# Log-sum-exp on one core: a second part of 16 rows per partition read last, the first logarithms held behind row 118, and more rows summed one by one

## The chip, the cores and the metric

The kernel runs on one core of a Trainium2 chip. The metric is the device time of one execution, in microseconds (us), the median of several runs. A profile is one further execution with the hardware profiler on; its span goes from the first to the last instruction, and some time lies around it.

## The reference

For each of 32 x 512 = 16384 rows of 1024 fp32 values the kernel computes the logarithm of the sum of exponentials:

```
max_x = np.max(x, axis=-1, keepdims=True)
return (max_x.squeeze(-1) + np.log(np.sum(np.exp(x - max_x), axis=-1))).astype(np.float32)
```

The input is 67.1 MB, drawn from a normal distribution. The output has 16384 fp32 values, 64 KB.

## The kernel before

The 16384 rows are spread over 128 partitions, 128 rows (columns of `sumexp`) to each. The kernel takes the exponentials without subtracting the maximum, sums them and takes the logarithm; beside this it finds out whether any sum left the range 1e-15 to 1e15, and only if one did does a second, careful pass run (the branch at L200, not taken with this input).

The rows lie in two parts of the input. `x_rest` has the last B = 8 rows per partition, `x_rows` the other W = 120. In either part a partition's rows are contiguous, so partitions begin 120 x 4 KB = 480 KB apart in the first and 32 KB apart in the second.

A list of 17 loads sets everything. Each load brings some rows of all partitions into the next free slots of a ring of 48 row slots in SBUF; when a load does not fit behind the last, it begins at slot 0 again. SyncE (SP) issues all loads on one queue (L90). Loads 2, 3 and 4 are issued as 4, 2 and 2 transfers, so that there are 22 in all. A transfer waits until the slots' former rows have been used, and the eight semaphores used for transfers are taken in turn, so that a transfer also waits until the eighth before it has landed.

The list gives each load's operations. A letter and a number stand for so many rows:

- `R8`: ScalarE takes the exponential of 8 rows in place (L133), and VectorE sums them with one reduction (L140).
- `T3`: ScalarE takes the exponential of 3 rows in place (L133), and VectorE sums row by row, with one instruction that adds the two halves of a row and sums the result (L145).
- `A`: ScalarE takes the exponential of one row and sums it in the same instruction (L131); VectorE has nothing to do.

The order of the instructions on each engine is made by a scheduler of the framework, which may put an instruction earlier than the program has it, and it makes the semaphore waits between engines from what each instruction reads and writes. Where the program knows a wait to be unneeded, it says so (`without_wait`).

Around the loads there are these steps:

- L162: the logarithms of the first EARLY = 104 columns, on ScalarE; L182: those of the last 24.
- L163 and L164: `check` of the first LATE = 118 columns: VectorE clamps the sums (L102), counts those that differ (L106), and TensorE adds the count into one PSUM value (L110). L188 does the same for columns 118 to 126.
- L183 and L184: two stores on SyncE's queue, first the 8 columns of `x_rest` (32 bytes per partition), at the end the 120 of `x_rows` (480 bytes). Load 7 is the one that reads `x_rest` (REST = 7), and its sums lie in columns 0 to 7.
- L189 to L195: VectorE looks at a part of the last row, TensorE adds this (L193) and the last row's sum (L194) to the count, and VectorE makes a flag of it (L195). ScalarE and VectorE load the flag and branch (L196 to L200). At L264 all engines finish together.

Of the kernel before, what the change touches and what calls it, by code (L numbers as in the profile page):

```python
# [14 lines left out]
def kernel(  # L15
# [5 lines left out]
    nc = tc.nc  # L21
# [3 lines left out]
    AF = mybir.ActivationFunctionType  # L25
# [6 lines left out]
    NC = n // P  # L32
# [2 lines left out]

    B = 8
    W = NC - B
    x_rows = x_flat[0 : P * W].rearrange("(p c) d -> p c d", p=P)  # L40
    x_rest = x_flat[P * W : n].rearrange("(p c) d -> p c d", p=P)
    out_flat = out.rearrange("a b -> (a b)")
    out_rows = out_flat[0 : P * W].rearrange("(p c) -> p c", p=P)
    out_rest = out_flat[P * W : n].rearrange("(p c) -> p c", p=P)
# [3 lines left out]

    RING = 48
    loads = [  # L50
        "R8 R8", "R8 R8", "R8 R8", "R7 R6 A A", "R6 R5 A A A", "R5 R4 A", "R5 R4", "R5 T3",
        "R3 A A A", "R3 A", "R2 T2", "R3", "R1 A", "T2", "T1", "A", "A",
    ]
    loads = [[(op[0], int(op[1:] or 1)) for op in load.split()] for load in loads]
    assert sum(s for ops in loads for _, s in ops) == NC
    ENGINES = [mybir.EngineType.Activation, mybir.EngineType.DVE]
    REST = 7
    EARLY = 104
    LATE = 118
    LAST = NC - 1  # L60

# [4 lines left out]
    ring = big.tile([P, RING, d], fp32, name="ring")  # L66
    sumexp = stats.tile([P, NC], fp32, name="sumexp")
    res = stats.tile([P, NC], fp32, name="res")
# [10 lines left out]
    nc.vector.memset(far, 100 * HIGH)  # L79

    def source(c0, size):
        assert c0 >= B or (c0 == 0 and size == B)
        return x_rows[:, c0 - B : c0 - B + size, :] if c0 >= B else x_rest

    def load(p0, c0, size, i):


        step = {2: 4, 3: 2, 4: 2}.get(i, 1)
        return [
            nc.sync.dma_start(  # L90
                out=ring[k::step, p0 : p0 + size, :], in_=source(c0, size)[k::step]
            ).ins
            for k in range(step)
        ]

    def without_wait(ins, group, reason):

        tc.declare_no_dep(ins.ins, group=group, reason=reason)


    def check(c0, c1, i):
        nc.vector.tensor_scalar(  # L102
            out=clamped[:, c0:c1], in0=sumexp[:, c0:c1],
            scalar1=LOW, scalar2=HIGH, op0=ALU.max, op1=ALU.min,
        )
        nc.vector.scalar_tensor_tensor(  # L106
            out=clamped[:, c0:c1], in0=clamped[:, c0:c1], scalar=0.0, in1=sumexp[:, c0:c1],
            op0=ALU.bypass, op1=ALU.not_equal, accum_out=bad[:, i : i + 1],
        )
        nc.tensor.matmul(count, lhsT=bad[:, i : i + 1], rhs=far, start=i == 0, stop=False)  # L110

    following = B
    p = 0
    for i, ops in enumerate(loads):
        size = sum(s for _, s in ops)
        if p + size > RING:
            p = 0
        if i == REST:
            c = 0
        else:  # L120
            c = following
            following += size
        dmas = load(p, c, size, i)
        if i == 0:
            first_load = dmas[0]
        for how, s in ops:
            v = ring[:, p : p + s, :]
            sums = sumexp[:, c : c + s]
            if how == "A":
                o = v if c < LAST else last_exp  # L130
                exp = nc.scalar.activation(out=o, in_=v, func=AF.Exp, accum_out=sums)  # L131
            else:
                exp = nc.scalar.activation(out=v, in_=v, func=AF.Exp)  # L133
            without_wait(exp, "loads", "the slot's earlier users came before this load")
            without_wait(exp, "exps", "the slot's earlier users came before this load")
            without_wait(exp, "sums", "the slot's earlier users came before this load")
            tc.add_to_no_dep_group("exps", exp.ins)
            added = []
            if how == "R":
                added = [nc.vector.reduce_sum(out=sums, in_=v, axis=AX.X)]  # L140
            elif how == "T":
                for r in range(s):
                    lo = ring[:, p + r, 0:H]
                    added.append(
                        nc.vector.scalar_tensor_tensor(  # L145
                            out=lo, in0=lo, scalar=1.0, in1=ring[:, p + r, H:d],
                            op0=ALU.mult, op1=ALU.add, accum_out=sums[:, r : r + 1],
                        )
                    )
            for add in added:  # L150
                for dma in dmas:
                    tc.declare_no_dep(add.ins, dma, reason="ScalarE has waited for it")
                without_wait(add, "loads", "they came before this one")
            for add in added:
                tc.add_to_no_dep_group("sums", add.ins)
            c += s
            p += s
            last_row = v
        for dma in dmas:
            tc.add_to_no_dep_group("loads", dma)  # L160
        if following == EARLY + 14:
            nc.scalar.activation(out=res[:, 0:EARLY], in_=sumexp[:, 0:EARLY], func=AF.Ln)  # L162
        if following == LATE + 3:  # L163
            check(0, LATE, 0)  # L164

    def start_early(program):

# [11 lines left out]

    nc.at_finalize(start_early)  # L180

    nc.scalar.activation(out=res[:, EARLY:NC], in_=sumexp[:, EARLY:NC], func=AF.Ln)  # L182
    nc.sync.dma_start(out=out_rest, in_=res[:, 0:B])  # L183
    nc.sync.dma_start(out=out_rows, in_=res[:, B:NC])  # L184

    check(LATE, LAST, 1)  # L188
    nc.vector.reduce_max(out=bad[:, 3:4], in_=last_row[:, 0, 0 : d // 16], axis=AX.X)  # L189
    nc.vector.tensor_scalar(  # L190
        out=bad[:, 2:3], in0=bad[:, 3:4], scalar1=LOG_LOW, scalar2=None, op0=ALU.is_lt
# [8 lines left out]
    with tc.If(all_fine < 1, preferred_fallthrough_block=False):  # L200
        with tc.tile_critical(sync_engine=mybir.EngineType.Activation):
            with nc.semaphore("landed") as landed, nc.semaphore("ready") as ready:
                rows = 0
                steps = 0
                for c0 in range(0, NC, RING):
                    s = min(RING, NC - c0)
                    v = ring[:, 0:s, :]
                    neg = clamped[:, c0 : c0 + s]
                    if c0:
                        nc.scalar.wait_ge(ready, steps)  # L210
                    for c1, s1 in ((0, B), (B, s - B)) if c0 == 0 else ((c0, s),):
                        nc.scalar.dma_start(
                            out=ring[:, c1 - c0 : c1 - c0 + s1, :], in_=source(c1, s1)
                        ).then_inc(landed, 16)
                        rows += 16
                    nc.vector.wait_ge(landed, rows)
                    nc.vector.tensor_reduce(
                        out=neg, in_=v, op=ALU.max, axis=AX.X, negate=True
                    ).then_inc(ready, 1)
                    nc.vector.wait_ge(ready, steps + 1)  # L220
                    nc.vector.tensor_add(
                        out=v, in0=v, in1=neg[:, :, None].to_broadcast([P, s, d])
                    ).then_inc(ready, 1)
                    nc.scalar.wait_ge(ready, steps + 2)
                    nc.scalar.activation(out=v, in_=v, func=AF.Exp).then_inc(ready, 1)
                    nc.vector.wait_ge(ready, steps + 3)
                    nc.vector.reduce_sum(
                        out=sumexp[:, c0 : c0 + s], in_=v, axis=AX.X
                    ).then_inc(ready, 1)
                    steps += 4  # L230
                nc.scalar.wait_ge(ready, steps)
                nc.scalar.activation(out=res, in_=sumexp, func=AF.Ln).then_inc(ready, 1)
                nc.vector.wait_ge(ready, steps + 1)
                nc.vector.tensor_sub(out=res, in0=res, in1=clamped).then_inc(ready, 1)
                nc.scalar.wait_ge(ready, steps + 2)
                nc.scalar.dma_start(out=out_rest, in_=res[:, 0:B]).then_inc(landed, 16)
                nc.scalar.dma_start(out=out_rows, in_=res[:, B:NC]).then_inc(landed, 16)
                nc.scalar.wait_ge(landed, rows + 32)


# [28 lines left out]
```

## Time and profile before

| | us |
|---|---|
| median of 4 runs | 163.75 (163.71 to 163.83) |
| the profiled execution | 163.94 |
| its span | 162.1 |
| VectorE busy | 122.4 (75%) |
| ScalarE busy | 116.8 (72%) |
| first exponential starts | 22.16 |
| last exponential starts | 158.30 |
| last logarithms start (L182) | 159.48 |
| final store (L184) issued | 159.73, lands 1.6 later |

The page's row of DMA tenths shows 40 equal slices of the span; a 9 is a slice in which the DMA engines were at least 90% busy. A group of instructions is shown by line, engine, operation, output and input, shape and count, then busy time and the mean length of one in ns, then the idle time of the engine just before them and what ended it. In a timeline a line begins with its start and length in us; the bracket tells how long the engine was idle before it and what it waited for. Neighbouring instructions of one form are merged into one line with their count.

### The profile page before, as it was taken

To read this page: it belongs to the slowest core of one execution; us is meant where nothing else is said; L and a number is where in the kernel's file an instruction comes from. 1 tells how busy PE (TensorE), PEld (TensorE's weight loads), DVE (VectorE), ACT (ScalarE), POOL (GpSimd) and SP (SyncE) were. 2 spreads that over 40 slices of the span, in tenths; PEclk is the share of its full clock that TensorE was granted. 3 is DMA by queue.
4 is the path that set the end of the run, shared out by engine and by line. 5 is a ranking of instruction groups with operands and counts; after the bars stand their busy time and mean duration, and the time that the engine had idled before them with its cause. 6 is when DMAs were issued, how large, how long until landed. Compare 5 with 4: busy or idle time off the path is not lost.

```text
span 162.1 us, 216 instructions
## 1 busy us (share of the span) xinstructions
PE 0.6 (0%) x8; PEld 0.3 (0%) x8; DVE 122.4 (75%) x47; ACT 116.8 (72%) x53; POOL 0.2 (0%) x4
## 2 busy tenths in 40 slices
PE   0000000000000000000000000000000000000001
PEld 0000000000000000000000000000000000000000
DVE  0000000799949999499999995999998999979993
ACT  3000059990799609994499839999969599999993
POOL 0000000000000000000000000000000000000000
DMA  8995996997997999699999979899999999999980
GB/s 259 517 517 259 517 517 275 501 517 307 469 517 340 437 501 470 273 470 485 453 453 453 439 338 434 384 443 437 437 412 485 398 418 416 437 409 417 417 329 17
DMA packets 2817, 67.18 MB, mean 414 GB/s; under 512 B 640, under 2 KB 640, under 8 KB 1024
## 3 DMA queue, kind: packets, MB, share of 16 engines
q1 hardware_dynamic: 2816, 67.18, 96.9%
q14 instruction: 1, 0.01, 0.0%
HBM read 67.11 MB, written 0.07 MB: 414 GB/s over the span
## 4 chain that ended last, share of the span: by engine, by line
DMA 63%; DVE 22%; ACT 12%; issue 0%; SPq 0%; PE 0%; DVEq 0%; ACTq 0%
DMA ring<-in_x_dram 63%; DVE sumexp L140 21%; ACT ring L133 12%; DVE ring L145 1%; SPq L90 0%; PE count L193 0%; DVE clamped L102 0%; DVE bad L190 0%; DVE bad L189 0%; DVE clamped L106 0%; DVE fine L195 0%; PE count L194 0%; DVEq L102 0%; ACTq L133 0%
## 5 line engine op out<-in xcount | busy, mean ns | idle before, releaser
L140 DVE TENSOR_REDUCE sumexp<-ring 128x8 f32<-128x8192 f32 (+7 forms) x20 | 116.2, 5855 | 36.1 <-ACT ring L133 36.1
L133 ACT ACTIVATE ring<-ring 128x8192 f32<-128x8192 f32 (+7 forms) x24 | 101.8, 4284 | 42.1 <-DMA ring<-in_x_dram 42.0
L131 ACT ACTIVATE ring<-ring 128x1024 f32<-128x1024 f32 x12 | 12.5, 1041 | 0.0
L145 DVE SCALAR_TENSOR_TENSOR ring<-ring 128x512 f32<-128x512 f32 x8 | 5.1, 687 | 0.0
L131 ACT ACTIVATION_READ_ACCUMULATOR ring<-ring 128x1 f32 x12 | 2.2, 187 | 0.0
L77 ACT ACT_TABLE_LOAD x1 | 1.3, 1283 | 0.8 <-PEq L253 0.8
L131 ACT ACTIVATE last_exp<-ring 128x1024 f32<-128x1024 f32 x1 | 1.0, 1027 | 0.0
L110 PE MATMUL count<-far,bad 128*1 128x1 f32 x4 | 0.4, 164 | 159.0 <-DVE clamped L106 159.0
L78 DVE MEMSET ones<- 128x1 f32 x1 | 0.1, 59 | 0.9 <-PEq L253 0.9
L145 DVE DVE_READ_ACCUMULATOR ring<-ring 128x1 f32 x8 | 0.7, 85 | 0.0
L106 DVE SCALAR_TENSOR_TENSOR clamped<-clamped,sumexp 128x118 f32<-128x118 f32 (+1 forms) x2 | 0.5, 226 | 0.1
L102 DVE TENSOR_SCALAR clamped<-sumexp 128x118 f32<-128x118 f32 (+1 forms) x2 | 0.4, 198 | 0.1
L110 PEld LDWEIGHTS count<-far,bad 128*1 128x1 f32 x4 | 0.2, 80 | 159.1 <-DVE clamped L106 159.1
L195 DVE TENSOR_SCALAR fine<-count 1x1 int32<-1x1 f32 x1 | 0.1, 146 | 0.3 <-PE count L194 0.3
L162 ACT ACTIVATE res<-sumexp 128x104 f32<-128x104 f32 x1 | 0.3, 273 | 0.0
L182 ACT ACTIVATE res<-sumexp 128x24 f32<-128x24 f32 x1 | 0.2, 223 | 0.0
L189 DVE TENSOR_REDUCE bad<-ring 128x1 f32<-128x64 f32 x1 | 0.2, 219 | 0.0
L193 PE MATMUL count<-far,bad 128*1 128x1 f32 x2 | 0.2, 164 | 0.2 <-DVE bad L190 0.2
L194 PE MATMUL count<-ones,sumexp 128*1 128x1 f32 x2 | 0.2, 163 | 0.0
L131 ACT ACTIVATION_READ_ACCUMULATOR last_exp<-ring 128x1 f32 x1 | 0.2, 186 | 0.0
L190 DVE TENSOR_SCALAR bad<-bad 128x1 f32<-128x1 f32 x1 | 0.2, 153 | 0.0
L106 DVE DVE_READ_ACCUMULATOR clamped<-clamped,sumexp 128x1 f32 x2 | 0.2, 84 | 0.0
(7 smaller groups left out, 0.7 us busy)
## 6 DMA issues: line engine op xcount, KB each, us to landing
ring<-in_x_dram SPq DMA_DIRECT2D x2, 3840.0 KB, 27.7
ring<-in_x_dram SPq DMA_DIRECT2D x2, 3584.0 KB, 25.6
ring<-in_x_dram SPq DMA_DIRECT2D x1, 5120.0 KB, 31.3
ring<-in_x_dram SPq DMA_DIRECT2D x1, 4608.0 KB, 33.7
ring<-in_x_dram SPq DMA_DIRECT2D x1, 4096.0 KB, 29.3
ring<-in_x_dram SPq DMA_DIRECT2D x2, 2048.0 KB, 32.7
ring<-in_x_dram SPq DMA_DIRECT2D x1, 3072.0 KB, 36.2
ring<-in_x_dram SPq DMA_DIRECT2D x2, 1024.0 KB, 38.8
```

The costliest lines, as they stand in the source:

```text
L77: nc.scalar.preload_act_table_set("natural_log_exp_and_others")
L102: nc.vector.tensor_scalar(out=clamped[:, c0:c1], in0=sumexp[:, c0:c1], scalar1=LOW, scalar2=HIGH, op0=ALU.max, op1=ALU.min,)
L106: nc.vector.scalar_tensor_tensor(out=clamped[:, c0:c1], in0=clamped[:, c0:c1], scalar=0.0, in1=sumexp[:, c0:c1], op0=ALU.bypass, op1=ALU.n ...
L110: nc.tensor.matmul(count, lhsT=bad[:, i : i + 1], rhs=far, start=i == 0, stop=False)
L131: exp = nc.scalar.activation(out=o, in_=v, func=AF.Exp, accum_out=sums)
L133: exp = nc.scalar.activation(out=v, in_=v, func=AF.Exp)
L140: added = [nc.vector.reduce_sum(out=sums, in_=v, axis=AX.X)]
L145: nc.vector.scalar_tensor_tensor(out=lo, in0=lo, scalar=1.0, in1=ring[:, p + r, H:d], op0=ALU.mult, op1=ALU.add, accum_out=sums[:, r : r + 1],
L162: nc.scalar.activation(out=res[:, 0:EARLY], in_=sumexp[:, 0:EARLY], func=AF.Ln)
L182: nc.scalar.activation(out=res[:, EARLY:NC], in_=sumexp[:, EARLY:NC], func=AF.Ln)
L189: nc.vector.reduce_max(out=bad[:, 3:4], in_=last_row[:, 0, 0 : d // 16], axis=AX.X)
L190: nc.vector.tensor_scalar(out=bad[:, 2:3], in0=bad[:, 3:4], scalar1=LOG_LOW, scalar2=None, op0=ALU.is_lt)
```

## The change

Five things are changed.

- B is 16 instead of 8, W 112 instead of 120, so partitions begin 448 KB apart in the first part and 64 KB apart in the second. Columns are now read in order, 0 to 127: the second part is columns 112 to 127 and is read last, by loads 9 to 16, where it was load 7.
- The list of loads is another: five loads of 16 rows and then 12, 8, 6, 6, 3, 3, 3, 2, 2, 1, 1, 1, where it was three of 16 and then 15, 14, 10, 9, 8, 6, 4, 4, 3, 2, 2, 1, 1, 1. 17 rows are summed one by one on VectorE (T) where 8 were, 10 on ScalarE (A) where 13 were.
- The first logarithms are those of 112 columns instead of 104. A new function, `in_this_order`, fixes an order on one engine without a wait: the logarithms stand behind the exponential of row 118 and ahead of the next one.
- The `check` of the first 118 columns is put ahead of the next sum on VectorE in the same way.
- The first store is that of the 112 columns of `x_rows` (448 bytes per partition), the final one that of the 16 of `x_rest` (64 bytes).

The branch that is not taken is changed to match.

```diff
-    B = 8
+    B = 16
...
     loads = [
-        "R8 R8", "R8 R8", "R8 R8", "R7 R6 A A", "R6 R5 A A A", "R5 R4 A", "R5 R4", "R5 T3",
-        "R3 A A A", "R3 A", "R2 T2", "R3", "R1 A", "T2", "T1", "A", "A",
+        "R6 R5 R5", "R6 R5 R5", "R8 R8", "R8 R8", "R4 R4 R3 R3 A A", "R6 T3 T3", "R6 A A", "T4 T2",
+        "R3 R3", "R3", "A A A", "R2 A", "T2", "T2", "T1", "A", "A",
     ]
...
-    REST = 7
-    EARLY = 104
     LATE = 118
...
-        assert c0 >= B or (c0 == 0 and size == B)
-        return x_rows[:, c0 - B : c0 - B + size, :] if c0 >= B else x_rest
+        assert c0 >= W or c0 + size <= W
+        return x_rest[:, c0 - W : c0 - W + size, :] if c0 >= W else x_rows[:, c0 : c0 + size, :]
...
+    def in_this_order(first, then):
+
+        info = mybir.DependencyInfo(mybir.DependencyClass.NoSync, mybir.DependencyReason.DATA)
+        tc.add_manual_dep(then.ins, first.ins.name, info, reason="order on one engine")
...
+            if ln:
+                in_this_order(ln, exp)
+                ln = None
...
+                if counted:
+                    in_this_order(counted, add)
+                    counted = None
...
-        if following == EARLY + 14:
-            nc.scalar.activation(out=res[:, 0:EARLY], in_=sumexp[:, 0:EARLY], func=AF.Ln)
-        if following == LATE + 3:
-            check(0, LATE, 0)
+        if c == LATE:
+            ln = nc.scalar.activation(out=res[:, 0:W], in_=sumexp[:, 0:W], func=AF.Ln)
+            in_this_order(exp, ln)
+            counted = check(0, LATE, 0)
...
-    nc.scalar.activation(out=res[:, EARLY:NC], in_=sumexp[:, EARLY:NC], func=AF.Ln)
-    nc.sync.dma_start(out=out_rest, in_=res[:, 0:B])
-    nc.sync.dma_start(out=out_rows, in_=res[:, B:NC])
+    nc.scalar.activation(out=res[:, W:NC], in_=sumexp[:, W:NC], func=AF.Ln)
+    nc.sync.dma_start(out=out_rows, in_=res[:, 0:W])
+    nc.sync.dma_start(out=out_rest, in_=res[:, W:NC])
```

More of the change, by code (lines that the diff above doesn't have):

```diff
@@ L105, in check @@
         )
-        nc.vector.scalar_tensor_tensor(
+        counted = nc.vector.scalar_tensor_tensor(
             out=clamped[:, c0:c1], in0=clamped[:, c0:c1], scalar=0.0, in1=sumexp[:, c0:c1],
@@ L110, in check @@
         nc.tensor.matmul(count, lhsT=bad[:, i : i + 1], rhs=far, start=i == 0, stop=False)
-    following = B
+        return counted
+    ln = counted = None
+    c = 0
     p = 0
@@ L117 @@
             p = 0
[L118 to L122, printed above, removed]
         dmas = load(p, c, size, i)
@@ L210 @@
                         nc.scalar.wait_ge(ready, steps)
-                    for c1, s1 in ((0, B), (B, s - B)) if c0 == 0 else ((c0, s),):
+                    edge = max(c0, min(W, c0 + s))
+                    for c1, c2 in ((c0, edge), (edge, c0 + s)):
+                        if c1 == c2:
+                            continue
                         nc.scalar.dma_start(
-                            out=ring[:, c1 - c0 : c1 - c0 + s1, :], in_=source(c1, s1)
+                            out=ring[:, c1 - c0 : c2 - c0, :], in_=source(c1, c2 - c1)
                         ).then_inc(landed, 16)
@@ L235 @@
                 nc.scalar.wait_ge(ready, steps + 2)
-                nc.scalar.dma_start(out=out_rest, in_=res[:, 0:B]).then_inc(landed, 16)
-                nc.scalar.dma_start(out=out_rows, in_=res[:, B:NC]).then_inc(landed, 16)
+                nc.scalar.dma_start(out=out_rest, in_=res[:, W:NC]).then_inc(landed, 16)
+                nc.scalar.dma_start(out=out_rows, in_=res[:, 0:W]).then_inc(landed, 16)
                 nc.scalar.wait_ge(landed, rows + 32)
```

## The prediction

> **What bounds the kernel now.** I read the page's line of busy DMA tenths and its queue line first, then the stages, then ScalarE's order of time from 119 us on, then what SyncE waits for at the end.
>
> ```profile
> DMA  8995996997997999699999979899999999999980
> q1 hardware_dynamic: 2816, 67.18, 96.9%
> ```
> ```profile
> 22.00:61.00 39.00, 0.00 (x0) 0.00 (x0) 29.70 (x4) 27.95 (x5) 0.00 (x0) 1.00 0.99 429
> 119.00:141.00 22.00, 0.00 (x0) 0.00 (x0) 21.54 (x11) 20.08 (x10) 0.00 (x0) 1.00 1.00 427
> 141.00:158.00 17.00, 0.19 (x2) 0.09 (x2) 15.78 (x17) 16.73 (x15) 0.00 (x0) 1.00 0.97 401
> 158.00:162.10 4.10, 0.43 (x6) 0.22 (x6) 1.43 (x10) 1.68 (x5) 0.00 (x0) 1.00 0.06 17
> ```
>
> In a stage line the columns after the length are PE, PEld, DVE, ACT and POOL busy, the clock, the DMA share and GB/s. The 16 DMA engines are full (0.97 to 1.00) in every stage until 158; of the 162.1 us the stream takes 157. So only three things can move the time: the stream itself, how far ScalarE and VectorE trail its last row, and the 4 us after it.
>
> ```profile
> 22.16 13.95 ACT L133 ACTIVATE ring<-ring 128x8192 f32<-128x8192 f32 x2 [20.08 <-DMA ring<-in_x_dram]
> 41.51 13.95 ACT L133 ACTIVATE ring<-ring 128x8192 f32<-128x8192 f32 x2 [5.40 <-DMA ring<-in_x_dram]
> 119.00 7.98 ACT L133 ACTIVATE ring<-ring 128x5120 f32<-128x5120 f32 x2 [1.27 <-DMA ring<-in_x_dram]
> 128.72 7.12 ACT L133 ACTIVATE ring<-ring 128x5120 f32<-128x5120 f32 x2 [1.75 <-DMA ring<-in_x_dram]
> 136.02 2.76 ACT L133 ACTIVATE ring<-ring 128x3072 f32<-128x3072 f32 x1 [0.18 <-DMA ring<-in_x_dram]
> 154.49 2.86 ACT L133 ACTIVATE ring<-ring 128x2048 f32<-128x2048 f32 x2 [0.23 <-DMA ring<-in_x_dram]
> 157.25 1.04 ACT L131 ACTIVATE ring<-ring 128x1024 f32<-128x1024 f32 x1
> 158.30 1.03 ACT L131 ACTIVATE last_exp<-ring 128x1024 f32<-128x1024 f32 x1
> 159.48 0.22 ACT L182 ACTIVATE res<-sumexp 128x24 f32<-128x24 f32 x1
> ```
>
> Each bracketed wait ends as a load lands, so differences of starts give the stream's law: 16 rows per partition 41.51 - 22.16 = 19.35 us, 6 rows 136.02 - 128.72 = 7.30 us, hence 1.205 us a row and 0.07 us a load. The last exponential starts at 158.30, straight behind its predecessor, and the trace's record of the last load's landing is 158.28: ScalarE arrives exactly as the data does.
>
> **The change, part by part.**
>
> *The stream.* Both schedules have 17 loads in 22 transfers, and both have brought 118 rows with load 10; from there both go 3, 2, 2, 1, 1, 1. By the law, row 118 lands at the same 145.8, the later loads at 149.5, 152.0, 154.5, 155.7, 157.0 and 158.3. Price 0, provided that each load is issued before the queue runs dry. The slots of the ring decide that, worked out with these prices (mean ns in the last but one place):
>
> ```profile
> L140 DVE TENSOR_REDUCE sumexp<-ring 128x6 f32<-128x6144 f32 x2 | 13.1, 6550 | 2.0 <-ACT ring L133 2.0
> L131 ACT ACTIVATE ring<-ring 128x1024 f32<-128x1024 f32 x12 | 12.5, 1041 | 0.0
> L133 ACT ACTIVATE ring<-ring 128x3072 f32<-128x3072 f32 x4 | 11.0, 2756 | 0.2 <-DMA ring<-in_x_dram 0.2
> L140 DVE TENSOR_REDUCE sumexp<-ring 128x3 f32<-128x3072 f32 x3 | 10.1, 3353 | 1.2 <-ACT ring L133 1.2
> L145 DVE SCALAR_TENSOR_TENSOR ring<-ring 128x512 f32<-128x512 f32 x8 | 5.1, 687 | 0.0
> ```
>
> From start to start they are a little shorter: an R6 sum 6.47, an R3 sum 3.27, a row summed alone 0.61 (138.63 to 139.24), exponentials 2.66 for three rows, 1.81 for two, 1.04 with their own sum. Load 5 (12 rows) needs load 2's two sums, which end at 85.4 as before; the stream wants it at 99.5. Load 6 needs load 3's first sum, 95.9, and is wanted at 114.0; load 7, 104.5 against 123.8; the last four wait for load 5's R6, 126.1, against 152. One more wait is SyncE's eight semaphores: a transfer waits for the eighth before it, so load 16 for load 8 (138.4, wanted at 157). Margins are 14 us and more: nothing shows.
>
> *Where the rows lie.* Partitions of the first part now begin 448 KB apart, not 480; those of the second 64 KB, not 32. The row that bears on this is the 8 rows before 128.72, the old second part: 9.72 us, where the law gives 9.71. Two very different distances agree within 0.1%, so I take 0, with 0.1% of the stream's 155 us, 0.16 us, either way. The Trainium skill, DMA: Bandwidth & Descriptors, section "Latency and other measured facts", speaks against the change: it has copies at a row pitch of 512 KiB at 207 GB/s where a padded layout reaches 214, blames large powers of two, and 448 KB is a multiple of 64 KB. If that 3% held here the time would be some 5 us longer; no run here shows such a loss.
>
> *ScalarE at the end.* Load 8 (R3 R3) lands at 138.40 and finds it idle. Then three R3 exponentials end at 146.40, A A A at 149.52, the 112 logarithms (0.18 until the next start, as the 104 took at 141.81) at 149.70, R2 151.51, A 152.55, T2 154.36. Load 13 lands at 154.48. From there the sequence T2, T1, A, A is the old one, so the last exponential again starts at 158.30. The cover is 0.13 us of idle time before load 13; any more delay than that goes one for one into the end.
>
> *What the logarithms wait for.* They need VectorE's sums through row 111 and stand in ScalarE's order, so a late sum holds up every exponential behind them, then VectorE's sums of those. VectorE by the prices above: load 4's four sums end at 119.65, R6 126.12, six single rows 129.78, R6 (its exponential ends at 129.95) 136.44, six single rows 140.1, then R3 from 141.2 to 144.47 and R3 to 147.8. That is 1.7 us before 149.52: price 0. The R3 of load 9 runs until 151.1, and the logarithms must not wait for it. The old ones started at 141.81 while a sum of rows they did not need ran from 140.46 to 143.8, so waits go by rows.
>
> *VectorE at the end.* The comparison of 118 rows (0.6 us) waits for load 10's A A A too (149.6, long past) and goes from 151.1 to 151.7; behind it stand R2, to 153.9, and nothing that ScalarE or a load waits for; T2 at 154.5 and T2 at 156.4 find it idle; T1 ends at 158.34 instead of 158.62. The nine single rows that replace sums of blocks cost 0.61 instead of 1.07 each, but in idle time.
>
> *The stores.* The first store now carries 448 bytes a partition and is queued behind all loads, as the 32-byte one was (16.4 us to landing); its eight packets an engine follow the last load and are done near 158.5, before the final store's first packet at 160.57. The final store shrinks from 480 to 64 bytes. In the packet records a 480-byte packet takes 26 ns and a 32-byte one 9; eight of each follow one another, 0.21 or 0.07 us. I take the nearer, 9: it lands 0.14 us earlier than 161.31; the bounds are 0 and 0.14.
>
> *What is late next.* SyncE's last waits:
>
> ```profile
> SPq L264 <- DVEq L200: 0.4, 1, 0.4
> SPq L264 <- DMA out_dram<-res: 0.3, 1, 0.3
> SPq L264 <- ACTq L200: 0.3, 1, 0.3
> ```
>
> The store's wait is only 0.3 us beyond the branch, and VectorE leaves the branch late: its closing drain is recorded at 161.35 to 161.40, SyncE's at 161.45. VectorE's side hangs on the flag, on PE L194, on the last sum at 159.46; PE's L193, until now held to 159.51 by VectorE's chain from the T rows, comes 0.27 us earlier, so L194 ends some 0.06 earlier. The closing barrier then follows 161.35 (VectorE) instead of 161.45: 0.10 us saved, not 0.14. Bounds 0 and 0.14.
>
> **Sum.** The profiled execution took 163.94 us, 162.1 in its span and 1.84 around it: 163.94 - 0.10 = 163.84. It lies 0.19 above the runs' median, so against that 163.75 - 0.10 = **163.65**. Less than 0.2% (0.33 us), about what a measurement of this kernel can tell from no change.
>
> **Rivals.**
> 1. *The logarithms wait for row 114* (slower). If the wait covers the R3 of load 9, ScalarE stands until 151.1, R2 ends at 153.1, A 154.1, T2 155.95, and load 13 starts 1.45 us after its landing; nothing behind it is idle, so the end moves by that: 163.65 + 1.45 = 165.1. It decides once the wait ends after 149.65. For it: 0.13 us of cover. Against: the old logarithms' start.
> 2. *The new addresses cost or the cover fails a little* (slower). Twice the 0.16 bound, or a hold of 0.5 us at the logarithms less 0.13, gives 164.0 to 164.2. For it: no row shows 448 KB; against: the law.
> 3. *The stream starts faster.* The first packets of 64 KB took 3.0 to 3.8 us by their records, later ones 2.42; their mean excess is 0.9 us. If it hangs on the addresses, the new ones may end it: down to 162.8. Against: it may be the start alone.
> 4. *The store does not shrink the end*: 26 ns a packet or the branch covers all: 163.75, indistinguishable.
>
> **Chances.** Forecast with rival 4: 0.60, 163.45 to 163.85. Rival 1: 0.10. Rival 2: 0.12. Rival 3: 0.18. So faster 0.18, same 0.60, slower 0.22. The range 163.1 to 164.3 leaves out rival 1 and the farther half of rival 3.
>
> **What would show it.** ScalarE's bracketed waits at the starts 138.4 and 154.5 in the new profile, and its last exponential at 158.30, show arrival unchanged; a VectorE wait before the logarithms, or load 13 starting after 154.5 with no DMA wait, shows rival 1. The first start of ScalarE (22.16) tells rival 3; steps of 19.35 us between 16-row loads tell rival 2. The final store's time to landing should be 1.4 us instead of 1.6. A DMA line with a slice below its neighbours between 60 and 150 us would make all of it wrong.

## The result, and the profile after

The changed kernel takes 164.14 us (median of 37 runs, 163.93 to 164.45), the kernel before 163.81 (57 runs, 163.65 to 164.11). The ratio is 1.0020, 95% interval 1.0016 to 1.0025: slower by a third of a microsecond, where 163.65 was forecast, a change too small to tell from none.

The page of the changed kernel, its row of DMA tenths and its queues (packets, MB, share of 16 engines):

```profile
DMA  7995997999899899799699598898899999999980
...
q1 hardware_dynamic: 2816, 67.18, 96.6%
q14 instruction: 2, 0.02, 0.0%
```

The load queue is as full as before (96.6% against 96.9%), so the stream is still the bound. The queue q14, by its name the one that brings the engines their own instructions, has two packets in the span. The page before has one:

```profile
q14 instruction: 1, 0.01, 0.0%
```

It looks like nothing: 0.02 MB of 67.

ScalarE in order of time, to be held against the lines of the prediction:

```profile
21.92 14.04 ACT L133 ACTIVATE ring<-ring 128x6144 f32<-128x6144 f32 x3 [19.84 <-DMA ring<-in_x_dram]
41.23 14.04 ACT L133 ACTIVATE ring<-ring 128x6144 f32<-128x6144 f32 x3 [5.27 <-DMA ring<-in_x_dram]
...
138.14 8.07 ACT L133 ACTIVATE ring<-ring 128x3072 f32<-128x3072 f32 x3 [1.10 <-DMA ring<-in_x_dram]
...
149.23 0.28 ACT L168 ACTIVATE res<-sumexp 128x112 f32<-128x112 f32 x1
...
157.41 1.06 ACT L131 ACTIVATE ring<-ring 128x1024 f32<-128x1024 f32 x1 [0.37 <-DMA ring<-in_x_dram]
158.37 0.19 ACT L131 ACTIVATION_READ_ACCUMULATOR ring<-ring 128x1 f32 x1
158.65 1.03 ACT L131 ACTIVATE last_exp<-ring 128x1024 f32<-128x1024 f32 x1
...
159.83 0.22 ACT L188 ACTIVATE res<-sumexp 128x16 f32<-128x16 f32 x1
```

Up to 155 us everything runs 0.2 to 0.3 earlier than in the kernel before or in the forecast, as the first exponential does (21.92 for 22.16): the first load landed earlier in this execution. The logarithms start with no wait in front of them. Then a wait appears that was in neither schedule: load 15, one row, makes ScalarE wait 0.37 us, and the last exponential starts at 158.65 instead of 158.30. The records of landings show why. A load lands in 16 parts, which I take to be one for each of the 16 DMA engines; 15 parts of load 15 landed between 156.34 and 156.73, the sixteenth at 157.38; of load 16, between 157.56 and 157.98, and the sixteenth at 158.63. In the loads before, the sixteenth part was never more than 0.09 us behind the fifteenth; now one DMA engine is 0.65 us behind its fellows. So the question is what held it.

The queues of both kernels in the window from 150 to 160 us, first before, then after:

```profile
q1 hardware_dynamic: 784, 3.02, 74.9%
```
```profile
q1 hardware_dynamic: 776, 3.01, 74.6%
q14 instruction: 1, 0.01, 0.2%
```

The kernel before has no line for q14 in this window. In the changed one an 8 KB packet of instructions runs at 155.61 to 155.94 by its record, and two 4 KB packets of the loads, the first of which starts as it ends, take 0.50 and 0.49 us instead of 0.16. In the kernel before the corresponding transfers came at 161.53 and 162.20, when no load was left to be delayed.

The final store did become shorter. Its line of issues (KB, us to landing) after:

```profile
out_dram<-res SPq DMA_DIRECT2D x1, 8.0 KB, 1.4
```

In the profiled pair the last exponential is 0.35 later and the store 0.15 shorter, together the 0.2 by which the spans differ (162.3 and 162.1).

### The profile page after: what moved, and what is told of

It is laid out like the page before. It is cut to its first block, busy times and chain, and to the rows that moved or that the text cites. A ratio compares the mean times of both kernels' runs of the same rounds, so it can differ in the third digit from the quotient of the medians.

```text
span 162.3 us, 231 instructions
## 1 busy us (share of the span) xinstructions
PE 0.8 (0%) x8; PEld 0.3 (0%) x8; DVE 121.5 (75%) x65; ACT 116.3 (72%) x50; POOL 0.2 (0%) x4
## 3 DMA queue, kind: packets, MB, share of 16 engines
q1 hardware_dynamic: 2816, 67.18, 96.6%
## 4 chain that ended last, share of the span: by engine, by line
DMA 66%; DVE 24%; ACT 8%; issue 1%; SPq 0%; PE 0%; ACTq 0%
DMA ring<-in_x_dram 66%; DVE sumexp L143 24%; ACT ring L133 8%; SPq L88 0%; ACT last_exp L131 0%; PE count L200 0%; DVE fine L201 0%; ACTq L133 0%
## 5 line engine op out<-in xcount | busy, mean ns | idle before, releaser
L143 DVE TENSOR_REDUCE sumexp<-ring 128x3 f32<-128x3072 f32 (+5 forms) x20 | 109.6, 5534 | 35.2 <-ACT ring L133 35.2
L133 ACT ACTIVATE ring<-ring 128x3072 f32<-128x3072 f32 (+6 forms) x27 | 104.4, 3921 | 42.4 <-DMA ring<-in_x_dram 42.4
L148 DVE SCALAR_TENSOR_TENSOR ring<-ring 128x512 f32<-128x512 f32 x17 | 10.7, 689 | 1.1 <-ACT ring L133 1.1
L131 ACT ACTIVATE ring<-ring 128x1024 f32<-128x1024 f32 x9 | 9.4, 1041 | 0.4 <-DMA ring<-in_x_dram 0.4
L131 ACT ACTIVATION_READ_ACCUMULATOR ring<-ring 128x1 f32 x9 | 1.7, 186 | 0.0
L148 DVE DVE_READ_ACCUMULATOR ring<-ring 128x1 f32 x17 | 1.4, 85 | 0.0
```

What stands on the lines that cost most here:

```text
L148: nc.vector.scalar_tensor_tensor(out=lo, in0=lo, scalar=1.0, in1=ring[:, p + r, H:d], op0=ALU.mult, op1=ALU.add, accum_out=sums[:, r : r + 1],
```

## The experiments

**The theory** of the code transfer: every row summed alone puts an addition and the reading of its accumulator into VectorE's program. In the profile after VectorE has 81 records, with its sequencer's waits and branches, where it had 61. By the theory it therefore comes to the end of a stored block of its program while the loads still run, the next block is fetched by one of the 16 full DMA engines, and that engine's share of every later load is late. **The rivals**: the new addresses cost; ScalarE's thin cover failed; any longer program costs.

### x1: fewer records on VectorE, all else as changed

```diff
-"R6 T3 T3"
+"R6 R3 A A A"
```

> The changed kernel with load 5 as R6 R3 A A A instead of R6 T3 T3: 11 fewer records on VectorE, all else (addresses, stores, order) as changed. Theory of the code transfer (VectorE reaches its 58th record while the loads still run, an 8 KB transfer of instructions then takes one DMA engine away for 0.65 us, and that engine's part of the last row comes late): that record is now reached near 158.9, after the last load; no instruction transfer between 0 and 158 us, all 16 landings of the last load within 0.5 us, time back to 163.4 to 163.75. Rival of the addresses (448 KB and 64 KB apart cost): 164.1 as changed. Rival of ScalarE's thin cover: its last exponentials still late by 0.3 us with more exponentials, 164.1 or more.

Measured: 163.62 us (11 runs), 0.9986 of the kernel before (0.9977 to 0.9995), 0.52 below the changed kernel. VectorE has 69 records instead of 81, twelve fewer (the expectation has eleven). From 150 to 160 us the load queue stands alone:

```profile
q1 hardware_dynamic: 792, 3.14, 77.0%
```

The transfers of instructions are at 161.41 and 161.61. All 16 parts of the last load landed between 157.83 and 158.17. ScalarE at the end:

```profile
154.34 2.86 ACT L133 ACTIVATE ring<-ring 128x2048 f32<-128x2048 f32 x2 [0.23 <-DMA ring<-in_x_dram]
...
158.19 1.03 ACT L131 ACTIVATE last_exp<-ring 128x1024 f32<-128x1024 f32 x1
```

The wait for the one-row load is gone and the end is that of the kernel before, 158.19 for 158.30. The addresses and stores are those of the changed kernel, so the addresses are acquitted; so is ScalarE, which works more here (116.7 us busy for 116.3). Another detail of the expectation was wrong too: the 58th record passed at 158.6 and no transfer was recorded until 161.4, so a count of records gives the place only roughly.

### x2: the records given back as fills

```diff
+    spare = stats.tile([P, 12], fp32, name="spare")
...
+    for k in range(12):
+        nc.vector.memset(spare[:, k : k + 1], 0.0)
```

> The kernel of x1 with 12 fills of one column each on VectorE before the first load has landed, when it is idle for 25 us (0.7 us of work). Theory of the code transfer: the 58th record is again reached near 155, the transfer lies in the stream again, 164.0 to 164.3, 0.3 to 0.6 above x1. Rivals of the addresses and of ScalarE: the fills are in idle time, the same as x1 within 0.1.

Measured: 164.17 us (ratio to before 1.0017, 1.0008 to 1.0026), 0.55 above x1. VectorE again has 81 records. An instruction packet is back in the stream, at 155.17, and two 4 KB packets behind it again take 0.50 and 0.49. The last load's sixteenth part landed at 158.67, the fifteenth at 158.24. ScalarE's last two exponentials:

```profile
157.44 1.06 ACT L134 ACTIVATE ring<-ring 128x1024 f32<-128x1024 f32 x1
...
158.69 1.03 ACT L134 ACTIVATE last_exp<-ring 128x1024 f32<-128x1024 f32 x1
```

Twelve instructions, executed some 150 us earlier on an idle engine, cost half a microsecond at the end. It isn't their time that costs: it is that what stands behind them in VectorE's program comes twelve instructions later.

### x3 and x5: the kernel before with the suspected part alone

x3 adds the fills, 20 of them, to the kernel before. x5 takes one part of the change alone, more rows summed one by one:

```diff
-"R5 R4 A", "R5 R4"
+"T5 R4 A", "T5 R4"
```

> The kernel before with 20 such fills at the start and nothing else. Theory of the code transfer: its 58th record comes near 152 us instead of 161, an instruction transfer falls into the stream and the kernel before becomes slower by 0.3 to 0.6 us: 164.1 to 164.4. Rivals: 163.8, the fills are free.

> The kernel before with loads 5 and 6 as T5 R4 A and T5 R4: of the change only its last part, ten more rows summed one by one, 18 more records on VectorE; ScalarE's and SyncE's orders stay. VectorE has less work (0.61 for 1.07 us a row). Theory of the code transfer: an instruction transfer falls into the stream near 153 us and the time goes from 163.85 to 164.2 to 164.7, although VectorE works less. Rival (single rows are harmless, the loss came from another part): 163.7 to 163.9.

Measured: x3 164.62 (1.0049, 1.0035 to 1.0063), x5 164.62 (1.0039, 1.0025 to 1.0053), each 0.77 above its 163.85 of the kernel before (5 runs each). The instruction packets are at 152.16 and 151.83. That is more than expected for x3 and the upper end for x5. The same packet costs 0.52 in the changed kernel; why it costs more here no run settles. ScalarE's last waits, x3 first:

```profile
155.20 2.86 ACT L136 ACTIVATE ring<-ring 128x2048 f32<-128x2048 f32 x2 [0.87 <-DMA ring<-in_x_dram]
...
159.00 1.00 ACT L134 ACTIVATE last_exp<-ring 128x1024 f32<-128x1024 f32 x1
```
```profile
155.21 2.85 ACT L133 ACTIVATE ring<-ring 128x2048 f32<-128x2048 f32 x2 [1.05 <-DMA ring<-in_x_dram]
...
159.01 1.00 ACT L131 ACTIVATE last_exp<-ring 128x1024 f32<-128x1024 f32 x1
```

The wait of 0.23 in front of load 13 grew to 0.87 and 1.05, and both last exponentials start 0.7 late. In x3 one 8 KB packet of a load takes 0.968 us instead of 0.312, in x5 the same: 0.66 us lost on one DMA engine. x5 removes work from VectorE, ten rows at 0.61 instead of 1.07, and is slower all the same.

### x4: the transfer 21 us earlier

The 20 fills in the changed kernel.

> The changed kernel with the 20 fills: the 58th record is reached near 138 instead of 155. If a delayed DMA engine keeps its delay to the end, because the queue is never empty, the time stays at 164.1 to 164.3; if the engine could catch up in 17 us, the time falls to 163.5 to 163.8. The rivals expect 164.1 as well, so this run only tells how long a delay lasts; the transfer's place in the records must move to 138 in the theory.

Measured: 164.11 us (1.0017, 1.0008 to 1.0027), the changed kernel's time. The instruction packet is at 134.47, earlier than the expected 138, and one 24 KB packet of a load right behind it takes 1.574 us instead of 0.913, again 0.66. From then on the sixteenth part of every load is 0.37 to 0.43 us behind the fifteenth, where it was 0.14; of the last load it landed at 158.50, the others by 158.13. The engine does not catch up in 23 us. That each of the 16 has a fixed share of every load and the queue is never empty would explain it; the records don't name the engine of a packet, so this is argued.

### x6: the fills on another engine

> The kernel before with the 20 fills of x3 on GpSimd instead of VectorE. If only an engine that comes to the end of its own stored instructions while the loads run matters, nothing changes: 163.7 to 163.95, no instruction transfer between 0 and 158 us. If any 20 instructions more in the program, or the fills themselves at the start, cost the 0.77 us of x3: 164.6.

Measured: 163.83 us (0.9997, 0.9988 to 1.0006), and no instruction packet before the loads' end. Neither a longer program nor the fills themselves cost anything; twenty instructions matter on VectorE and not on GpSimd. The record of a packet does not name the engine it brings instructions to. That it is VectorE follows from x2, x3 and x8, where fills on VectorE alone move the packet or add one.

### x8: two transfers

> The changed kernel with 128 fills at the start. If one transfer of 8 KB brings 128 instructions, there are two in the stream, the first within the fills before 10 us and the second near 155 where the changed kernel has its one. A DMA engine never catches up, so two transfers on one DMA engine give 164.1 + 0.66 = 164.8, on different engines 164.1 to 164.3. If the place is not set by the count of VectorE's instructions: one transfer, 164.1.

Measured: 164.99 us (1.0071, 1.0057 to 1.0084), 0.85 above the changed kernel, somewhat more than the 0.66 expected for one engine. The instruction queue from 2 to 150 us and from 150 to 160 us:

```profile
q14 instruction: 1, 0.01, 0.0%
```
```profile
q14 instruction: 1, 0.01, 0.2%
```

The packets are at 6.64 and 155.53; the second is where the changed kernel has its first, 128 instructions of VectorE further. The 64 KB packet behind the first takes 2.948 us instead of 2.418, and two 4 KB packets behind the second 0.49 and 0.48: 0.53 and 0.66 us lost. Both fell on the same DMA engine by the landings, in which one part alone is late: 0.39 to 0.42 us behind the fifteenth in every load from 22 to 155 us, and in load 16, of which 15 parts landed by 158.16, at 159.48, 1.32 behind. ScalarE's end shows it as a gap in front of each one-row load (0.38, then 0.13 and 0.10):

```profile
157.06 1.06 ACT L136 ACTIVATE ring<-ring 128x1024 f32<-128x1024 f32 x1 [0.38 <-DMA ring<-in_x_dram]
158.25 1.06 ACT L134 ACTIVATE ring<-ring 128x1024 f32<-128x1024 f32 x1
...
159.50 1.03 ACT L134 ACTIVATE last_exp<-ring 128x1024 f32<-128x1024 f32 x1
```

### x9: the transfer just behind the last load

> The kernel of x1 with 6 fills instead of the 12 of x2. In x1 the 58th record passed at 158.6 with no transfer until 161.4, so the count of records alone does not tell the place. If the place moves with VectorE's instructions, it is now near 158, where the last row's packets are done or nearly: 163.5 to 163.8, as x1. If any few fills bring the transfer well into the stream: 164.0 to 164.3, as x2.

Measured: 163.66 us (0.9988, 0.9979 to 0.9997), as x1. The transfers are at 159.67 and 161.37: six fills moved one from 161.4 to 159.67, later than the expected 158 but in the gap between the last load and the packets of the final store, where it costs nothing. With 0, 6 and 12 fills the first transfer lies at 161.41, 159.67 and 155.17. It moves with VectorE's program, and it costs once it falls among the loads.

### x7: without the fixed order

The kernel of x1 without the calls of `in_this_order`, those for the logarithms and that for the `check`; the scheduler puts the logarithms three instructions earlier.

```diff
-            in_this_order(exp, ln)
...
-                in_this_order(ln, exp)
...
-                    in_this_order(counted, add)
```

> The kernel of x1 without the fixed order (logarithms behind the exponential of row 118, the comparison ahead of the next sum): the scheduler then puts the 112 logarithms ahead of load 10's A A A, near 146.1, where they have to wait for VectorE's sum of row 111, which ends near 147.5. Rival 1 of the prediction, with its price: ScalarE stands 1.4 us, nothing behind it is idle for more than some 0.1, the end moves by 1.2 to 1.4 us: 164.8 to 165.1. If the wait is covered: 163.6 as x1.

Measured: 164.91 us (1.0070, 1.0056 to 1.0084), 1.29 above x1.

```profile
147.60 0.30 ACT L162 ACTIVATE res<-sumexp 128x112 f32<-128x112 f32 x1 [1.38 <-DVE sumexp L140]
...
159.35 1.00 ACT L131 ACTIVATE last_exp<-ring 128x1024 f32<-128x1024 f32 x1
```

The bracket names it: ScalarE waits 1.38 us for VectorE's sum of row 111, and 1.16 of that is left at the last exponential (159.35 against 158.19). The fixed order is worth 1.3 us to this list of loads.

### x10: both stores last

```diff
+    in_this_order(rest_store, rows_store)
```

where `rest_store` is the final store of the 16 columns and `rows_store` that of the 112.

> The kernel of x1 with the store of 112 columns put behind the final one, so that both are issued after the last logarithms; nothing else. If the landing of the final store sets the end, the second store is issued 0.35 to 0.4 later and lands 0.15 later than a small one: 164.05 to 164.2. If the branch of VectorE and ScalarE covers the stores (rival 4 of the prediction): 163.6 to 163.75.

Measured: 164.08 us (1.0013, 1.0004 to 1.0022), 0.46 above x1. SyncE's last waits, x1 first, then x10:

```profile
SPq L273 <- DVEq L206: 0.8, 1, 0.8
SPq L273 <- PEq L273: 0.6, 2, 0.4
```
```profile
SPq L274 <- PEq L274: 0.6, 2, 0.4
SPq L274 <- DMA out_dram<-res: 0.6, 1, 0.6
SPq L274 <- DVEq L207: 0.3, 1, 0.3
```

With the small store alone SyncE's last long wait is for VectorE's branch; with a second store behind it, it is again for a landing. The two sides of the tail lie close together, as the prediction had them.

x1 and x9 beat both kernels, the kernel before by some 0.2 us.

## Why the prediction was wrong, point by point

**The bound** was right: the load stream, then the trailing engines, then the tail.

**The step that failed is "The stream", with its price of 0** "provided that each load is issued before the queue runs dry". The loads were issued in time; what was not asked is who else uses the 16 DMA engines. The step on VectorE's end failed with it: the nine single rows "cost 0.61 instead of 1.07 each, but in idle time". Their time was as said, and T1 even ended at 158.04 instead of the forecast 158.34, but each also brings instructions (VectorE has 20 more records in all), to which the prediction gave no price. In place of 0 stand 0.52 us (changed kernel against x1) and 0.55 (x2 against x1); in the kernel before a transfer costs 0.77 (x3, x5). The page before had a q14 line with one packet, and its record, at 161.53, some 3 us past the loads, could have raised the question; the prediction left it out.

**The addresses** at 0 were right: loads of 16 rows start 41.23 - 21.92 = 19.31 us apart after, 19.35 before, and x1 has the new addresses. The Trainium skill (DMA: Bandwidth & Descriptors, "Latency and other measured facts") has copies between HBM tensors at 207 GB/s with a row pitch of 512 KiB and at 214 with a padded one. That loss, an estimated 3% from these two figures, does not appear here. The row is about large powers of two, and 448 KB is none.

**ScalarE's order** was right: the forecast starts of 138.4 and 149.52 came at 138.14 and 149.23, both earlier by about what the first load was. The cover before load 13 held as well: T2, T2 and T1 take 4.78 us from 152.25 in the changed kernel and 4.64 in x7, where they run without a gap, so 0.14 us of idle time is left, 0.13 forecast. The changed kernel first:

```profile
152.25 4.78 ACT L133 ACTIVATE ring<-ring 128x2048 f32<-128x2048 f32 x3
```
```profile
153.76 4.64 ACT L133 ACTIVATE ring<-ring 128x2048 f32<-128x2048 f32 x3
```

**Rival 1** did not happen: the logarithms started at 149.23 without a wait, while VectorE was still at the last of these sums, rows 112 to 114, which they do not need:

```profile
140.93 9.87 DVE L143 TENSOR_REDUCE sumexp<-ring 128x3 f32<-128x3072 f32 x3 [1.02 <-ACT ring L133]
```

Its price was tried in x7, with the wait brought about by the order: 1.29 us, where the prediction's form of it gave 1.45.

**The tail**: 1.4 us to landing as forecast. Without the transfer x1 gains 0.23 us (0.08 to 0.38 by the interval) where 0.10 was forecast; the interval holds both, so how far 0.10 was short stays open. That gain is not shown to come from the store. Rival 4 in its strong form, a tail that hides the stores altogether, falls with x10, where the last landing comes 0.43 later than in x1 (161.46 for 161.03) and the time 0.46; whether the shorter store alone shortened the end no run tells, for in x1 the long wait is for the branch.

**The range** of 163.1 to 164.3 held 164.14, but by luck: rival 2's 164.0 to 164.2 stood for addresses and cover, and neither cost anything. (Its two prices give 163.97 and 164.02; 164.2 follows from neither.)

## What to carry to other kernels

Where the DMA engines are full from the first load to the last, count VectorE's instructions as well as its time: a form that is faster per row but needs two instructions for each can push a fetch of program code into the stream, and its delay stays to the end. Look for the instruction queue in windows of the trace, not in its share of the span, which was 0.0% here. If a fetch can't be avoided, a few instructions more or less can decide whether it falls among the loads or behind them (0, 6 and 12 fills here).

## What the runs showed of the hardware

- A recorded instruction packet of 8 KB lasts 0.33 us but costs the DMA engine it falls on 0.66 us: 0.968 for 0.312 in x3, 1.574 for 0.913 in x4, two packets of 0.50 and 0.49 for 0.16 each in the changed kernel; 0.53 behind the first one of x8. Why it is twice the packet's length no run tells.
- The delay is not made up within 23 us of full queue (x4), nor in x8 within 130 (0.39 to 0.42 us behind from 22 to 155 us), and two on one engine add: 1.32 us in x8.
- Between the second instruction packet of x8 and the first of the changed kernel lie 128 fills and 0.08 us, and one packet more came. So 128 instructions make up a whole block; at 8 KB that would be 64 bytes each, an estimate from these two numbers.
- The Trainium skill (Runtime: NRT & Kernel Launch, "Instruction fetch mechanics") says that crossing a block of the program costs one push of a DMA queue's tail and is mostly hidden. VectorE itself shows no wait for it in the changed kernel; the cost fell on the loads, 0.5 to 0.8 us of the kernel's time. The page gives blocks of 16 KiB, 256 instructions; the records here show packets of 8 KB, and x8 a step of 128.
- What exactly sets the place of a transfer stays open: it came after 54 to 58 of VectorE's records in five kernels (the changed one, x2, x3, x4, x5) and in the kernel before, but after 66 in x1 and x9, which differ from x2 only in the number of fills.
